# Softmax numerators divided ahead of their transposes, and the products with the values column-tiled for two heads

## The chip, the cores and the metric

The kernel runs on one core of one Trainium2 chip. The metric is the time of one execution in device microseconds (us); less is better. The kernel before took 598.86 us, the median of three runs (598.07 to 598.87 us).

## The reference

Two layers of a hybrid block work on a sequence of 256 tokens, 1024 wide, all in float32. Each layer has three mixers side by side: six heads of block attention ("moba", which on 256 tokens is one causal block), four heads of a chunked mLSTM, and six heads of sliding-window attention ("swa", window 128, two key heads, a sink in the softmax). Their outputs go through w_out, and a feed-forward part with a squared ReLU follows. Cut to what matters here:

```python
def moba_attention(q, k, v):            # causal over 256 tokens
    s = einsum('bhqd,bhld->bhql', q, k) * D ** -0.5
    p = softmax(where(k_pos <= q_pos, s, -inf))
    return einsum('bhql,bhld->bhqd', p, v)

def swa_attention(q, k, v, sinks):      # window of 128, q in two blocks
    s = where(mask, einsum('bnqkgd,bnjkd->bnkgqj', qb, kb) * D ** -0.5, -inf)
    p = softmax(concatenate([s, sink]))[..., :-1]
    return einsum('bnkgqj,bnjkd->bnqkgd', p, vb)

def hybrid_layer(x, ...):
    hn = rms_norm(x, ln1); proj = hn @ w_in      # q, k, v of all mixers
    ...
    x = x + concatenate([y_moba, y_mlstm, y_swa]) @ w_out
    return x + square(relu(rms_norm(x, ln2) @ w_up)) @ w_down
```

## The kernel before

**Large products.** Each float32 product with a weight matrix is made as three passes in a reduced format (fp32r): both operands are split into a high part and the rest, and `three` (L734) issues high times high, high times rest, rest times high (L736, L737, L738). A weight piece comes in by DMA as `raw`; `split` (L289) writes its high part `whi` on ScalarE (L267) and the rest `wlo` on VectorE (L274). There are 8 `whi` and 7 `wlo` buffers, so the splits run ahead of TensorE by at most that much.

**Attention.** `pair` (L1227) handles two heads: six pairs in each layer, three swa and three moba. It makes the scores of both heads in two banks of PSUM (L1249, plain float32, two row tiles of 64 rows side by side). For 256 queries and 256 keys only three of four blocks of 128 are needed, so a head's scores are 128x384: block (0,0), then (1,0) and (1,1). `head` (L1296) then masks and scales them and takes the row's extreme on VectorE (L1312, two instructions a head, called ISA in the order of instructions), takes the exponential on ScalarE with the sum of each row as a by-product (L1318), transposes the three blocks on TensorE (`to_T`, L805, L813) and copies them back to SBUF on ScalarE (L1329). With both heads there, `values` (L1263) multiplies the transposed numerators, as stationary operand, with the values of 64 columns: six products a pair (L1269). The result has the queries on partitions, so the division comes behind it: one reciprocal (L1281) and one product on VectorE (L1284, recorded as L274, out of PSUM); for swa the sinks are added to the sums before. Then two transposes (L813) turn the result, and `split` writes it as high part and rest (`fh`, `fl`) for w_out.

**The rest of a layer.** `mix` (L1336) multiplies with w_out: four results of 128x512, each over eight pieces in the order 3, 4, 5, 6, 7, 0, 1, 2 (the mLSTM's, swa's, moba's). Behind it `turn_both` (L697) transposes the new x (L708) for the feed-forward part, and `hT`, `lT` are its two parts. In the first layer `small_loads` (L586) then loads the second layer's small table by DMA into `tab` and makes `cg` and `sg` from it on VectorE (L597).

**What sets the order.** Nothing is ordered at run time. `Scheduler.run` (L164) builds the program: each piece of work is a generator that yields operations with an engine and a cost in us, and the planner issues the one that can start first by its own clock. Among those that are ready within a few hundredths of a us the lowest rank goes first. Two rules touch the change. Before a long operation on ScalarE or VectorE it looks a little ahead for an urgent one (rank of -25 or less), L213 to L218. An operation with an alternative engine takes the one that ends first, with 0.3 us of favour for the first (`choose`, L95). For TensorE a change of tile mode counts as 0.2 us. Each engine executes its list in order, so an instruction that waits holds all behind it.

Of the kernel before, what the change touches and what calls it, by code (L numbers as in the profile page):

```python
# [14 lines left out]
AF = mybir.ActivationFunctionType  # L15
# [6 lines left out]
HD = 64  # L22
# [113 lines left out]
class Scheduler:  # L136
# [27 lines left out]
    def run(self):  # L164
        while self.threads:
# [47 lines left out]
            if eng in ("ACT", "DVE") and op.cost > 0.3 and th.rank() > URGENTLY:  # L213

                soon = [c for c in ready if c[2].engine == eng and c[1].rank() <= URGENTLY
                        and t < c[0] < min(t + 0.5, t + op.cost - 0.2)]
                if soon:
                    t, th, op = min(soon, key=lambda c: c[0])  # L218
# [25 lines left out]
def tile_hybrid_block(ctx: ExitStack, tc: tile.TileContext, x, xT, smalls, w_in, w_out, w_up,  # L244
# [28 lines left out]
    def tt(waits, o, a, b, op):  # L273
        return dve(waits, free_size(o), lambda: V.tensor_tensor(o, a, b, op=op), bank=bank_of(a, b))  # L274
# [11 lines left out]
    def pe(waits, cost, fn, tiles=""):  # L286
        return Op("PE", cost, waits, fn, tiles=tiles)
# [317 lines left out]
    def small():  # L605
        i, t = yield Get(SMALL)
        return i, SMALL.tiles[i], t
# [237 lines left out]
    class Layer:  # L845
# [381 lines left out]
        def pair(self, swa, i, gate, prio):  # L1227
# [3 lines left out]

# [24 lines left out]
            i4, sums, t4 = yield from small()  # L1256
            for n, (h, (ip, _)) in enumerate(zip(heads, banks)):
                sch.add(prio + h, self.head(swa, h, n, pT, sums, done, ip, max(t, t4)))
# [4 lines left out]
            def values():  # L1263
                for qb in range(2):
                    for n, h in enumerate(heads):
                        d = (n if swa else h) * HD
                        for kb in range(qb + 1):
                            c = (qb + kb) * 128
                            T.matmul(yps[:, qb * 128 + n * HD:qb * 128 + n * HD + HD],  # L1269
                                     MID.tiles[pT[h]][:, c:c + 128], vv[kb][:, d:d + HD],  # L1270
                                     start=kb == 0, stop=kb == qb)

            t = yield pe([done, ty, vev], 0.68, values).ranked(prio)
# [4 lines left out]
            w = [t]  # L1278
            if swa:
                w = [t, (yield tt([done], sums[:, 0:4], sums[:, 0:4], sums[:, 4:8], OP.add))]  # L1280
            tr = yield dve(w, 16, lambda: V.reciprocal(sums[:, 0:4], sums[:, 0:4]))  # L1281
            im, tm = yield Get(MID)
            y = MID.tiles[im][:, 0:256]
            t = yield tt([t, tr, tm], y.rearrange("p (g d) -> p g d", d=HD),  # L1284
                         yps[:, 0:256].rearrange("p (g d) -> p g d", d=HD),
                         sums[:, 0:4, None].to_broadcast([128, 4, HD]), OP.mult)
            PS.put(iy, t)
            SMALL.put(i4, t)
            iy, ps, t = yield from to_T(t, y, 2)
            MID.put(im, t)  # L1290
            hi, lo, ty = yield from self.y_tile(c)
            t = yield from split([t, ty], hi, lo, ps[:, 0:256])
# [3 lines left out]
        def head(self, swa, h, n, pT, sums, done, ip, t):  # L1296
# [5 lines left out]
            nm = sm[:, 0:2]  # L1302
# [14 lines left out]
            for k, cut in enumerate(cuts):  # L1317
                t = yield act([tk], p[:, cut], p[:, cut], AF.Exp, bias=nm[:, k:k + 1],  # L1318
                              scale=-1.0, accum_out=sums[:, 2 * k + n:2 * k + n + 1])
            te = t  # L1320
            if swa:
                es = sums[:, 4:8].rearrange("p (b n) -> p b n", n=2)
                te = yield act([tk], es[:, :, n], nm, AF.Exp,
                               bias=tab[self.l][:, T_SINK + h:T_SINK + h + 1])
            SMALL.put(i, te)
# [6 lines left out]
            done.signal(max(t, te))  # L1332
# [361 lines left out]
```

## Time and profile before

| | |
|---|---|
| median of three runs | 598.86 us |
| time of the profiled execution | 598.18 us |
| its span, first to last instruction | 596.4 us |
| TensorE (PE) busy | 587.6 us, 99% |
| VectorE (DVE) busy | 523.2 us, 88% |
| ScalarE (ACT) busy | 382.3 us, 64% |
| granted TensorE clock | 1.000 |

PE is the matrix engine, PEld its weight loads, which run beside the products. An operation has a line of the kernel, the tiles that it writes and reads (`ps` is a bank of PSUM), and its shape. A float32 product is two records in the profile, because it is done in two passes; a transpose and an fp32r product are one. A matmul's recorded time includes its way through the array, so the distance between two starts says what it costs, not its length. Idle time stands in brackets, with what ended it. Attention lies at about 60 to 115 us in the first layer and 348 to 410 us in the second; each is followed by the feed-forward part.

### The profile page before, as it was taken

To read this page: it belongs to the slowest core of one execution; us is meant where nothing else is said; L and a number is where in the kernel's file an instruction comes from. 1 tells how busy PE (TensorE), PEld (TensorE's weight loads), DVE (VectorE), ACT (ScalarE), POOL (GpSimd) and SP (SyncE) were. 2 spreads that over 40 slices of the span, in tenths; PEclk is the share of its full clock that TensorE was granted. 3 is DMA by queue.
4 is the path that set the end of the run, shared out by engine and by line. 5 is a ranking of instruction groups with operands and counts; after the bars stand their busy time and mean duration, and the time that the engine had idled before them with its cause. 6 is when DMAs were issued, how large, how long until landed. Compare 5 with 4: busy or idle time off the path is not lost.

```text
span 596.4 us, 11480 instructions
## 1 busy us (share of the span) xinstructions
PE 587.6 (99%) x4327; PEld 550.4 (92%) x4327; DVE 523.2 (88%) x1153; ACT 382.3 (64%) x745; POOL 6.8 (1%) x14
## 2 busy tenths in 40 slices
PE   8999999989999999999999999999999999999997
PEld 6999998889999999999999999988999999999996
DVE  6899988389998998989899999875999998998995
ACT  6956887567574656546586778865766555555560
POOL 4000000000000000000000000000000000000000
PEclk9999999999999999999999999999999999999999
DMA  9937236255766466565555453353536556566422
GB/s 318 355 87 241 72 124 199 67 161 177 232 205 210 171 210 209 162 207 198 154 156 161 125 165 126 105 180 109 208 143 225 199 185 211 171 202 218 145 71 71
DMA packets 40967, 103.48 MB, mean 174 GB/s; under 512 B 3568, under 2 KB 17648, under 8 KB 40912
## 3 DMA queue, kind: packets, MB, share of 16 engines
q1 hardware_dynamic: 40496, 102.21, 52.6%
q8 instruction: 34, 0.56, 0.4%
q0 software_dynamic: 128, 0.40, 0.2%
q10 hardware_dynamic: 288, 0.15, 0.1%
q14 instruction: 21, 0.17, 0.1%
HBM read 101.69 MB, written 1.05 MB: 172 GB/s over the span
## 4 chain that ended last, share of the span: by engine, by line
PE 93%; ACT 2%; DMA 2%; DVE 1%; SPq 0%; issue 0%; DVEq 0%; ACTq 0%
PE ps L736 28%; PE ps L738 28%; PE ps L737 28%; PE ps L813 3%; PE ps L1269 3%; PE ps L1249 2%; DMA xs<-in_x_dram 1%; ACT whi L267 1%; DMA mid<-in_xT_dram 1%; DVE wlo L274 1%; ACT tmp L267 1%; PE ps L1056 1%; ACT hT L267 0%; DVE xs L274 0%; PE ps L1031 0%; PE ps L1078 0%
## 5 line engine op out<-in xcount | busy, mean ns | idle before, releaser
L274 DVE TENSOR_TENSOR wlo<-raw,whi 128x1024 fp32r<-128x1024 f32 (+4 forms) x240 | 223.8, 951 | 6.4 <-ACT whi L267 4.4
L267 ACT ACTIVATE whi<-raw 128x1024 fp32r<-128x1024 f32 (+4 forms) x240 | 189.5, 838 | 1.7 <-DMA raw<-in_w_in_dram 1.2
L738 PE MATMUL ps<-hT,wlo 128*128 128x256 f32 x576 | 161.4, 280 | 1.5 <-DVE wlo L274 1.5
L736 PE MATMUL ps<-hT,whi 128*128 128x256 f32 x576 | 162.1, 281 | 0.0
L737 PE MATMUL ps<-lT,whi 128*128 128x256 f32 x576 | 161.6, 281 | 0.0
L736 PE MATMUL ps<-whi,fh 128*128 128x256 f32 (+1 forms) x418 | 140.9, 337 | 0.0
L738 PE MATMUL ps<-whi,fl 128*128 128x256 f32 (+1 forms) x418 | 138.8, 332 | 0.0
L737 PE MATMUL ps<-wlo,fh 128*128 128x256 f32 (+1 forms) x418 | 138.8, 332 | 0.0
L738 PEld LDWEIGHTS ps<-hT,wlo 128*128 128x128 f32 x576 | 108.6, 188 | 1.8 <-DVE wlo L274 1.8
L736 PEld LDWEIGHTS ps<-hT,whi 128*128 128x128 f32 x576 | 108.6, 188 | 0.9
L737 PEld LDWEIGHTS ps<-lT,whi 128*128 128x128 f32 x576 | 108.5, 188 | 0.8
L738 PEld LDWEIGHTS ps<-whi,fl 128*128 128x128 f32 x418 | 78.6, 188 | 8.3
L736 PEld LDWEIGHTS ps<-whi,fh 128*128 128x128 f32 x418 | 78.7, 188 | 6.8 <-issue 0.7
L737 PEld LDWEIGHTS ps<-wlo,fh 128*128 128x128 f32 x418 | 78.7, 188 | 6.2
L267 ACT ACTIVATE arena<-ps 128x512 f32<-128x512 f32 (+3 forms) x52 | 26.3, 515 | 86.7 <-PE ps L738 81.6
L736 PE MATMUL ps<-whi,hT 128*128 128x256 f32 (+2 forms) x256 | 79.9, 312 | 0.7 <-ACT whi L267 0.6
L737 PE MATMUL ps<-wlo,hT 128*128 128x256 f32 (+2 forms) x256 | 76.1, 297 | 1.2 <-DVE wlo L274 1.2
L738 PE MATMUL ps<-whi,lT 128*128 128x256 f32 (+2 forms) x256 | 75.6, 295 | 0.0
L267 ACT ACTIVATE fh<-arena 128x1024 fp32r<-128x1024 f32 x32 | 34.0, 1062 | 48.2 <-DVE arena L274 44.4
L274 DVE TENSOR_TENSOR arena<-arena 128x128 f32<-128x128 f32 (+1 forms) x158 | 55.8, 360 | 4.5 <-ACT arena L267 3.7
L736 PEld LDWEIGHTS ps<-whi,hT 128*128 128x128 f32 x256 | 48.2, 188 | 3.4 <-issue 1.7
L737 PEld LDWEIGHTS ps<-wlo,hT 128*128 128x128 f32 x256 | 48.3, 189 | 2.1 <-DVE wlo L274 2.1
(141 smaller groups left out, 687.3 us busy)
## 6 DMA issues: line engine op xcount, KB each, us to landing
raw<-in_w_up_dram SPq DMA_DIRECT2D x64, 512.0 KB, 4.6
raw<-in_w_down_dram SPq DMA_DIRECT2D x64, 512.0 KB, 4.3
raw<-in_w_in_dram SPq DMA_DIRECT2D x24, 512.0 KB, 4.7
raw<-in_w_out_dram SPq DMA_DIRECT2D x16, 512.0 KB, 3.4
raw<-in_w_in_dram SPq DMA_DIRECT2D x16, 384.0 KB, 3.9
raw<-in_w_in_dram SPq DMA_DIRECT2D x7, 520.0 KB, 5.1
xs<-in_x_dram SPq DMA_DIRECT2D x2, 512.0 KB, 7.2
mid<-in_xT_dram SPq DMA_DIRECT2D x7, 128.0 KB, 5.5
```

The source lines that it names most:

```text
L267: lambda: A.activation(o, i, func, **kw), bank)
L274: return dve(waits, free_size(o), lambda: V.tensor_tensor(o, a, b, op=op), bank=bank_of(a, b))
L736: T.matmul(ps, s[0], m[0], start=start, stop=False)
L737: T.matmul(ps, s[0], m[1], start=False, stop=False)
L738: T.matmul(ps, s[1], m[0], start=False, stop=stop)
L813: T.transpose(ps[:, cs], src[:, cs], ident)
L1056: T.matmul(PS.tiles[ip][:, o], lqk[b, 2 + c, ks], lqk[b, c, qs], start=o.start == 0, stop=o.start > 0)
L1249: T.matmul(PS.tiles[ip][:, o], qT[b, i, q], kT[b, kc, k], start=o.start == 0, stop=o.start > 0)
L1269: T.matmul(yps[:, qb * 128 + n * HD:qb * 128 + n * HD + HD], MID.tiles[pT[h]][:, c:c + 128], vv[kb][:, d:d + HD], start=kb == 0, stop=kb = ...
```

## The change

The sum of a row's exponentials is now used before the transposes. Each head takes its two reciprocals (for swa, after adding the sink's exponentials), multiplies both parts of its numerators by them, on VectorE or, where that ends sooner by the planner's clock, on ScalarE, and only then transposes. The product with the values swaps its operands: the values (64 columns) are stationary, the transposed probabilities move, and the two heads write partitions 0 to 63 and 64 to 127 of one bank, each in a column tile of its own. The result so has the head's dimension on partitions, as w_out wants it: the division behind, its buffer and the two transposes are gone, and `split` reads the bank. The cost that the planner takes for the product stays 0.68 us; the tile mode "columns" is new to it, so that each change to and from it counts as 0.2 us. The look-ahead for urgent operations is cut from 0.5 to 0.3 us, and the least remainder raised from 0.2 to 0.3 us.

```diff
@@ Scheduler.run
                 soon = [c for c in ready if c[2].engine == eng and c[1].rank() <= URGENTLY
-                        and t < c[0] < min(t + 0.5, t + op.cost - 0.2)]
+                        and t < c[0] < min(t + 0.3, t + op.cost - 0.3)]
@@ pair
-            i4, sums, t4 = yield from small()
-            for n, (h, (ip, _)) in enumerate(zip(heads, banks)):
-                sch.add(prio + h, self.head(swa, h, n, pT, sums, done, ip, max(t, t4)))
+            for h, (ip, _) in zip(heads, banks):
+                sch.add(prio + h, self.head(swa, h, pT, done, ip, t))
...
             def values():
-                for qb in range(2):
+                for o, blk, cols in ((slice(0, 256), 0, slice(0, 256)),
+                                     (slice(128, 256), 1, slice(256, 384))):
                     for n, h in enumerate(heads):
                         d = (n if swa else h) * HD
-                        for kb in range(qb + 1):
-                            c = (qb + kb) * 128
-                            T.matmul(yps[:, qb * 128 + n * HD:qb * 128 + n * HD + HD],
-                                     MID.tiles[pT[h]][:, c:c + 128], vv[kb][:, d:d + HD],
-                                     start=kb == 0, stop=kb == qb)
-
-            t = yield pe([done, ty, vev], 0.68, values).ranked(prio)
+                        T.matmul(yps[64 * n:64 * n + 64, o], vv[blk][:, d:d + HD],
+                                 MID.tiles[pT[h]][:, cols], start=blk == 0, stop=blk == 1)
+
+            t = yield pe([done, ty, vev], 0.68, values, "columns").ranked(prio)
...
-            w = [t]
-            if swa:
-                w = [t, (yield tt([done], sums[:, 0:4], sums[:, 0:4], sums[:, 4:8], OP.add))]
-            tr = yield dve(w, 16, lambda: V.reciprocal(sums[:, 0:4], sums[:, 0:4]))
-            im, tm = yield Get(MID)
-            y = MID.tiles[im][:, 0:256]
-            t = yield tt([t, tr, tm], y.rearrange("p (g d) -> p g d", d=HD),
-                         yps[:, 0:256].rearrange("p (g d) -> p g d", d=HD),
-                         sums[:, 0:4, None].to_broadcast([128, 4, HD]), OP.mult)
-            PS.put(iy, t)
-            SMALL.put(i4, t)
-            iy, ps, t = yield from to_T(t, y, 2)
-            MID.put(im, t)
             hi, lo, ty = yield from self.y_tile(c)
-            t = yield from split([t, ty], hi, lo, ps[:, 0:256])
+            t = yield from split([t, ty], hi, lo, yps[:, 0:256])
@@ head
             for k, cut in enumerate(cuts):
                 t = yield act([tk], p[:, cut], p[:, cut], AF.Exp, bias=nm[:, k:k + 1],
-                              scale=-1.0, accum_out=sums[:, 2 * k + n:2 * k + n + 1])
-            te = t
+                              scale=-1.0, accum_out=su[:, k:k + 1])
             if swa:
-                es = sums[:, 4:8].rearrange("p (b n) -> p b n", n=2)
-                te = yield act([tk], es[:, :, n], nm, AF.Exp,
-                               bias=tab[self.l][:, T_SINK + h:T_SINK + h + 1])
-            SMALL.put(i, te)
+                te = yield act([tk], es, nm, AF.Exp, bias=tab[self.l][:, T_SINK + h:T_SINK + h + 1])
+                t = yield tt([te, t], su, su, es, OP.add)
+            t = yield dve([t], 16, lambda: V.reciprocal(su, su))
+            tn = []
+            for k, cut in enumerate(cuts):
+                a, b = p[:, cut], su[:, k:k + 1]
+                tn.append((yield ts([t], a, a, b, None, OP.mult).either(
+                    act([t], a, a, AF.Copy, scale=b))))
+            t = max(tn)
+            SMALL.put(i, t)
             it, pt, t = yield from to_T(t, p, 3)
...
-            done.signal(max(t, te))
+            done.signal(t)
```

Over the whole program TensorE has 48 products for the values where 72 stood, and 24 transposes fewer. VectorE gets 24 reciprocals for 12, 12 additions of the sinks for 6, and 42 of the 48 scalings, and loses 12 products out of PSUM; ScalarE gets the other 6 scalings. The lists of SyncE and GpSimdE are the same as before. On TensorE nothing moves ahead of the first layer's attention; in the attention and the feed-forward part's start of both layers much is ordered anew, and different buffers are used.

**TensorE, the last moba pair of the first layer.** `mid_78` and `mid_79` are the transposed numerators of its two heads (after: `mid_83` and `mid_79`), `arena` holds the values, `fh`, `fl` are the mixers' results. Before:

```order
L1269 MATMUL ps_65<-arena,mid_78 128x64
L1269 MATMUL ps_65<-arena,mid_79 128x64
L1269 MATMUL ps_65<-arena,mid_78 128x64 x2
L1269 MATMUL ps_65<-arena,mid_79 128x64 x2
L736 MATMUL ps_70<-whi_93,fh_107 128x512
L737 MATMUL ps_70<-wlo_104,fh_107 128x512
L738 MATMUL ps_70<-whi_93,fl_111 128x512
L736 MATMUL ps_70<-whi_94,fh_108 128x512
L737 MATMUL ps_70<-wlo_105,fh_108 128x512
L738 MATMUL ps_70<-whi_94,fl_112 128x512
L813 MATMUL ps_66<-ident,mid_84 128x128 x2
```

The same place now:

```order
L1266 MATMUL ps_65<-mid_83,arena 64x256
L1266 MATMUL ps_65<-mid_79,arena 64x256
L1266 MATMUL ps_65<-mid_83,arena 64x128
L1266 MATMUL ps_65<-mid_79,arena 64x128
L736 MATMUL ps_67<-whi_99,fh_107 128x512
L737 MATMUL ps_67<-wlo_103,fh_107 128x512
L738 MATMUL ps_67<-whi_99,fl_111 128x512
L736 MATMUL ps_70<-whi_95,fh_108 128x512
L737 MATMUL ps_70<-wlo_106,fh_108 128x512
L738 MATMUL ps_70<-whi_95,fl_112 128x512
```

Six products became four, and the two transposes of the divided result (`mid_84`) are gone.

**VectorE, the same pair's softmax.** The ISA rows mask the scores and take the row's extreme; `small` holds extremes, sums and reciprocals. Before, it goes on with the division of the pair ahead and with weight splits:

```order
L1312 ISA mid_82,small_118<-ps_65,masks,rq_m 128x256
L1312 ISA small_118 128x1
L1312 ISA mid_83,small_132<-ps_66,masks,rq_m 128x256
L1312 ISA small_132 128x1
L1281 RECIPROCAL small_134<-small_134 128x4
L274 TENSOR_TENSOR mid_84<-ps_65,small_134 128x256
L274 TENSOR_TENSOR wlo_104<-raw_88,whi_92 128x1024
```

Now:

```order
L1295 ISA mid_80,small_125<-ps_65,masks,rq_m 128x256
L1295 ISA small_125 128x1
L1306 RECIPROCAL small_124<-small_124 128x2
L278 TENSOR_SCALAR mid_76<-mid_76,small_124 128x128
L278 TENSOR_SCALAR mid_76<-mid_76,small_124 128x256
L1306 RECIPROCAL small_125<-small_125 128x2
L278 TENSOR_SCALAR mid_80<-mid_80,small_125 128x128
L278 TENSOR_SCALAR mid_80<-mid_80,small_125 128x256
L274 TENSOR_TENSOR fl_111<-ps_66,fh_107 128x256
L274 TENSOR_TENSOR wlo_104<-raw_88,whi_92 128x1024
```

Each head has a reciprocal and two scalings behind its exponentials, and the rest of an earlier pair's result (`fl_111`) and a weight split are queued behind them.

**VectorE, the start of the first layer's feed-forward part.** `lT` is the rest of the turned x, `wlo_101` the fourth weight piece that TensorE needs there, and `cg` is made from the second layer's table. Before:

```order
L283 SCALAR_TENSOR_TENSOR lT<-ps_66,tab,hT 128x256 x2
L274 TENSOR_TENSOR small_133<-small_133 128x1
L274 TENSOR_TENSOR arena<-raw_89 128x256
L278 TENSOR_SCALAR stat_148<-small_133 128x1
L597 SCALAR_TENSOR_TENSOR cg<-rope_t,tab 128x128
L274 TENSOR_TENSOR wlo_101<-raw_86,whi_96 128x1024
```

Now:

```order
L283 SCALAR_TENSOR_TENSOR lT<-ps_65,tab,hT 128x256
L283 SCALAR_TENSOR_TENSOR lT<-ps_63,tab,hT 128x256
L274 TENSOR_TENSOR wlo_101<-raw_86,whi_96 128x1024
L278 TENSOR_SCALAR stat_148<-stat_148 128x1
L274 TENSOR_TENSOR arena<-raw_90,arena 128x256
L274 TENSOR_TENSOR wlo_102<-raw_87,whi_97 128x1024
L597 SCALAR_TENSOR_TENSOR cg<-rope_t,tab 128x128
```

The splits into `wlo_101` and `wlo_102` now stand ahead of the first `cg`.

More of the change, by code (lines that the diff above doesn't have):

```diff
@@ L1277, in pair, with head @@
             gate.put(ig, t)
-            w = [t]
-            if swa:
-                w = [t, (yield tt([done], sums[:, 0:4], sums[:, 0:4], sums[:, 4:8], OP.add))]
-            tr = yield dve(w, 16, lambda: V.reciprocal(sums[:, 0:4], sums[:, 0:4]))
-            im, tm = yield Get(MID)
-            y = MID.tiles[im][:, 0:256]
-            t = yield tt([t, tr, tm], y.rearrange("p (g d) -> p g d", d=HD),
-                         yps[:, 0:256].rearrange("p (g d) -> p g d", d=HD),
-                         sums[:, 0:4, None].to_broadcast([128, 4, HD]), OP.mult)
-            PS.put(iy, t)
-            SMALL.put(i4, t)
-            iy, ps, t = yield from to_T(t, y, 2)
-            MID.put(im, t)
             hi, lo, ty = yield from self.y_tile(c)
-            t = yield from split([t, ty], hi, lo, ps[:, 0:256])
+            t = yield from split([t, ty], hi, lo, yps[:, 0:256])
             PS.put(iy, t)
             self.y[c].signal(t)
-        def head(self, swa, h, n, pT, sums, done, ip, t):
+        def head(self, swa, h, pT, done, ip, t):
             ps = PS.tiles[ip]
@@ L1301, in head @@
             i, sm, t0 = yield from small()
-            nm = sm[:, 0:2]
+            nm, su, es = sm[:, 0:2], sm[:, 2:4], sm[:, 4:6]
             cuts = (slice(0, 128), slice(128, 384))
```

## The prediction

> **What bounds the kernel now.** I read the page's head and its chain first, then what TensorE waits for.
>
> ```profile
> span 596.4 us, 11480 instructions
> PE 587.6 (99%) x4327; PEld 550.4 (92%) x4327; DVE 523.2 (88%) x1153; ACT 382.3 (64%) x745; POOL 6.8 (1%) x14
> PE 93%; ACT 2%; DMA 2%; DVE 1%; SPq 0%; issue 0%; DVEq 0%; ACTq 0%
> PE ps L738 <- DVE wlo L274: 1.5, 1, 1.5
> ```
>
> TensorE is busy for 99% of the span and is 93% of the chain that ended last. The answer on TensorE's waits has five rows, the longest is shown; none names an attention line (L813, L1249, L1269). So inside attention TensorE waits for nobody, and what its list there loses or gains is lost or gained at the end, as long as no wait comes in. What its pieces cost, the chain in order of time and the timeline of TensorE say:
>
> ```profile
> 61.71 1.51 PE ps L1249 x16
> 64.65 0.86 PE ps L1249 x8
> 80.45 1.28 PE ps L1269 x12
> 81.74 0.33 PE ps L813 x3
> ```
>
> ```profile
> 64.37 0.28 PE L738 MATMUL ps<-whi,lT 128*128 128x256 f32 x1
> 64.58 0.93 PE L1249 MATMUL ps<-arena 64*128 64x128 f32 x8
> 65.44 0.39 PE L736 MATMUL ps<-whi,hT 128*128 128x256 f32 x1
> 65.66 0.28 PE L737 MATMUL ps<-wlo,hT 128*128 128x256 f32 x1
> ...
> 77.89 0.37 PE L736 MATMUL ps<-whi,hT 128*128 128x256 f32 x1
> 78.09 0.29 PE L737 MATMUL ps<-wlo,hT 128*128 128x256 f32 x1
> 78.22 0.29 PE L738 MATMUL ps<-whi,lT 128*128 128x256 f32 x1
> ```
>
> A pair's values take 1.28 us (twelve records), a transpose 0.33/3 = 0.11 us. Of the weight products of 256 columns each starts 0.13 us behind the last (78.09 to 78.22), but the second behind a plain float32 group starts 0.20 us behind the first (77.89 to 78.09): leaving such a group costs 0.07 us, 0.08 with the rounding. Behind the row-tiled scores it is 0.22 us (65.44 to 65.66), and the scores start 0.21 us behind the last weight product (64.37 to 64.58): entering a tile mode costs about 0.09 us, leaving it 0.10.
>
> **What goes from TensorE.** Twelve pairs of values: 12 x 1.28 = 15.4 us. The 24 transposes of the results: 24 x 0.11 = 2.6 us. In the lists of both programs a run of weight products follows something else 81 times before and 69 times after: 12 x 0.08 = 1.0 us. Together 19.0 us.
>
> **What comes.** No row shows column tiles. The nearest is the scores: the same two heads, the same 256 and 128 moving columns, two tiles side by side, eight records. One pair takes 0.86 us and two pairs 1.51 us, so a pair streams for 1.51 - 0.86 = 0.65 us, and 0.21 us come once for a group. That gives the bounds for one new group: 0.65 us where even the 0.21 is hidden, 0.86 us as the scores, and 0.65 + 0.65 + 0.21 = 1.51 us where the two heads' tiles take turns. I take 0.86, since streams, heads and passes are those of the scores: 12 x 0.86 = 10.3 us. Entering and the dearer leaving, 0.09 + 0.02 us in twelve places at most: 1.3 us (none, if column tiles switch for free). From the Trainium skill, "TensorE: Matmul & The Clock Gate", section "Measured speedup vs the span model": three column tiles gained 2.38 times, 0.79 of their number; by that, as an estimate, two tiles would take 1.30/1.59 = 0.82 us of streaming beside the 0.21, and the sum would come out 2 us higher.
>
> So TensorE's own list shrinks by 19.0 - 10.3 - 1.3 = 7.4 us.
>
> **The stall at the first layer's feed-forward part.** The one long wait is this, in the timelines of TensorE and of VectorE:
>
> ```profile
> 129.51 0.28 PE L737 MATMUL ps<-lT,whi 128*128 128x256 f32 x1
> 131.33 0.39 PE L738 MATMUL ps<-hT,wlo 128*128 128x256 f32 x1 [1.55 <-DVE wlo L274]
> ```
>
> ```profile
> 126.25 0.86 DVE L283 SCALAR_TENSOR_TENSOR lT<-ps,tab,hT 128x256 fp32r<-128x256 f32 x2
> ...
> 129.85 0.29 DVE L597 SCALAR_TENSOR_TENSOR cg<-rope_t,tab 128x128 f32<-128x128 f32 x1 [2.27 <-DMA tab<-in_smalls_dram]
> 130.06 1.22 DVE L274 TENSOR_TENSOR wlo<-raw,whi 128x1024 fp32r<-128x1024 f32 x1
> ```
>
> VectorE stands 2.27 us at the first `cg`, which waits for the table's DMA, and the split that TensorE needs is queued behind it. TensorE starts 131.33 - 129.51 = 1.82 us later instead of 0.13, so 1.7 us are lost. In the new order that split and the next stand ahead of `cg`. The table's DMA lands 129.85 - 127.11 = 2.7 us behind the last `lT`; in the new list VectorE has two splits and two small operations there, about 1.2 + 1.2 + 0.4 us, so `cg` hardly waits. Late next is `wlo_101` itself. Its new row stands behind two transposed halves and two other splits, but TensorE has 12 weight products of the last mix (12 x 0.24 us, by the distance of 512-wide starts further below, 107.69 to 107.93) between the transposes, which it lacked before. I take 1.5 of the 1.7 us as won, with 0 and 1.9 as ends.
>
> **What is longer in the softmax.** A head's transposes now wait for a reciprocal and two scalings, for swa for the sink's exponential and an addition as well. The groups of instructions price them by the nearest shapes:
>
> ```profile
> L278 DVE TENSOR_SCALAR tmp<-tmp,tab 128x256 f32<-128x256 f32 x8 | 3.2, 402 | 0.0
> L1281 DVE RECIPROCAL small<-small 128x4 f32<-128x4 f32 x12 | 2.0, 171 | 2.3 <-ACT mid L267 2.3
> L274 DVE TENSOR_TENSOR small<-small 128x4 f32<-128x4 f32 x6 | 0.9, 152 | 0.0
> L267 ACT ACTIVATE small<-small,tab 128x2 f32<-128x2 f32 x12 | 3.4, 284 | 0.0
> ```
>
> The scaling of 256 is at most 0.40 us (that row has two per-row operands, the new one has one), that of 128 lies between the 0.15 us of the smallest operations and 0.40; I take 0.28. A moba head's chain grows by 0.17 + 0.28 + 0.40 = 0.85 us, a swa head's by 0.28 + 0.15 more, 1.3 us. What covers it can be read at the first layer's last pair, where least other work is left:
>
> ```profile
> 107.69 0.40 PE L737 MATMUL ps<-wlo,fh 128*128 128x512 f32 x1
> 107.93 0.39 PE L738 MATMUL ps<-whi,fl 128*128 128x512 f32 x1
> ...
> 111.27 0.49 PE L813 MATMUL ps<-ident,mid 128*128 128x128 f32 x3
> ```
>
> ```profile
> 109.82 0.18 ACT L267 ACTIVATION_READ_ACCUMULATOR mid<-mid,small 128x1 f32 x1
> ```
>
> The second head is ready at 109.82 + 0.18 = 110.00, and its transposes start 1.27 us later: 0.85 us would fit without moving anything. And it moves: in the new list twelve 512-wide products and one values group lie between this pair's scores and its first transposes, 12 x 0.24 + 1.06 = 3.9 us, where 12 x 0.24 + 0.1 = 3.0 us lay. Elsewhere the new transposes are put later by similar amounts. On VectorE the reciprocal that waits for the exponentials has `fl_111` and a weight split queued behind it, but there VectorE stood idle for 4.25 us:
>
> ```profile
> 114.47 0.42 DVE L274 TENSOR_TENSOR mid<-ps,small 128x256 f32<-128x256 f32 x1 [4.25 <-PE ps L1269]
> ```
>
> I charge 0.5 us for single short waits, 0 to 3 us.
>
> VectorE's load: 42 scalings by 0.34 us on the mean, 12 reciprocals by 0.17 and 6 additions by 0.15 more, less 12 of the products out of PSUM above by 0.42: 14.3 + 2.0 + 0.9 - 5.0 = 12 us, 6 in each layer. These stages of the first layer hold it:
>
> ```profile
> 60.00:75.00 15.00, 15.00 (x127) 13.91 (x125) 14.96 (x73) 13.07 (x49) 0.00 (x0) 1.00 0.23 75
> 75.00:90.00 15.00, 15.00 (x132) 14.13 (x130) 12.92 (x43) 13.40 (x41) 0.00 (x0) 1.00 0.39 134
> 90.00:105.00 15.00, 15.00 (x100) 12.94 (x96) 12.51 (x36) 10.60 (x31) 0.00 (x0) 1.00 0.61 193
> 105.00:115.00 10.00, 10.00 (x58) 8.02 (x57) 2.47 (x11) 4.57 (x13) 0.00 (x0) 1.00 0.09 34
> ```
>
> The fourth number is VectorE's: idle 2.1 + 2.5 + 7.5 = 12 us from 75 to 115 us, twice what is added; only from 60 to 75 is it full. I count nothing. The look-ahead alone moves nothing on TensorE ahead of attention and is in the order read above: nothing either.
>
> **The sum.** -7.4 - 1.5 + 0.5 = -8.4 us against the profiled execution's 598.18 us: 589.8 us. The median before lies 0.68 us above that execution; I give 590.0.
>
> **The rivals.**
> 1. *The column tiles take turns.* Both tiles use all rows of the array. Then a group takes 1.51 us, 12 x 0.65 = 7.8 us more: 597.6 us, about what it was. For it: nothing here shows two column tiles at once. Against: two row tiles do run at once. The Trainium skill, "TensorE: Matmul & The Clock Gate", section "The mechanism", speaks for it: weight loads pass running matmuls only where the row group differs, and here it doesn't. The trace disagrees, in groups:
>
> ```profile
> L1269 PE MATMUL ps<-arena,mid 128*128 128x64 f32 x144 | 17.4, 270 | 0.0
> L1269 PEld LDWEIGHTS ps<-arena,mid 128*128 128x128 f32 x144 | 17.3, 191 | 0.4
> ```
>
> Loads and products on all 128 rows fill 17.3 and 17.4 us, but one pair's twelve are through in 1.28 us, 15.4 us for all: they overlap. Chance 0.12.
> 2. *The longer softmax takes TensorE's place.* In-order TensorE stands at each head's transposes until VectorE has scaled. The 24 heads' chains grow by 12 x 0.85 + 12 x 1.3 = 26 us; the change turns into a loss once more than 8.9/24 = 0.37 us a head stay uncovered, and with half of it uncovered the time is 598.18 - 8.9 + 13 = 602.3 us. Against: the 1.27 us above, and the order. Chance 0.08.
> 3. *VectorE's added work comes too early for its idle time.* It is full from 60 to 75 us; if the 6 us a layer push the weight splits into TensorE's way, all 12 come back: 589.8 + 12 = 601.8 us. It decides where the splits are less than 6 us ahead. Against: VectorE later runs out of work (2.47 of 10 us), so the splits are then as far ahead as their buffers let them. Chance 0.05.
>
> My forecast has 0.75.
>
> **How the numbers follow.** The forecast's own ends: with 0.65 us a group (-2.5), free switching (-1.3), 586.0; with the stall kept (+1.5) and 3 us of waits (+2.5), 593.8. For 8 in 10 part of the rivals is needed, as 0.25 us a head uncovered (+6): 586 to 596. A measurement of this kernel tells 0.2%, 1.2 us, from no change. Faster: the forecast 0.75, and milder forms of the rivals, 0.04 + 0.02 + 0.02, together 0.83. Same: 0.08 of rival 1. Slower: 0.06 + 0.03 = 0.09.
>
> **What would show it.** Right: eight records of values per pair in 0.86 us (0.65 to 0.9), starts in pairs; no wait of TensorE on L813 beyond 0.5 us in all; no 1.5 us wait for `wlo` behind 120 us; a span of about 588 us. Rival 1 would show as 1.5 us a pair and starts one by one; rival 2 as waits of L813 for L278; rival 3 as waits for `wlo` in attention. Wrong altogether would be a loss in the feed-forward part, whose order changes little.

## The result and the profile after

| | before | after |
|---|---|---|
| median of the runs on one chip | 598.87 us (598.07 to 599.72, 4 runs) | 588.68 us (588.53 to 589.14, 4 runs) |
| profiled execution, its span | 598.18, 596.4 us | 588.58, 586.8 us |
| TensorE busy | 587.6 us | 579.8 us |
| VectorE busy | 523.2 us | 528.1 us |

The ratio is 0.9831 [0.9814, 0.9848]: the change is 1.7% faster. The prediction said 590.0 us (586 to 596).

The page's head after, its chain by engine, and TensorE's waits (the whole answer):

```profile
span 586.8 us, 11358 instructions
PE 579.8 (99%) x4255; PEld 538.9 (92%) x4255; DVE 528.1 (90%) x1200; ACT 384.9 (66%) x752; POOL 6.8 (1%) x14
PE 95%; DMA 3%; DVE 1%; SPq 0%; issue 0%; ACT 0%; DVEq 0%
```

```profile
PE ps L557 <- DVE mid L551: 1.1, 1, 1.1
PE ps L736 <- ACT whi L267: 0.7, 1, 0.7
PE ps L737 <- DVE wlo L274: 0.6, 2, 0.4
PE ps L737 <- DVE lT L283: 0.4, 1, 0.4
PE ps L879 <- DVE stat L283: 0.2, 1, 0.2
```

TensorE still sets the end. The 1.5 us wait of L738 is gone, no attention line is among the waits, and one wait is new: L737 for `lT`. The chain in order of time shows the new values (L1266, in before L1269 with 1.28 us) beside the scores (L1248):

```profile
81.58 1.45 PE ps L1266 x16
85.01 0.80 PE ps L1266 x8
85.81 0.86 PE ps L1248 x8
```

A pair takes 0.80 us; two pairs behind each other take 1.45 us, so a pair streams for 0.65 us. In the trace its eight records start in four couples, 7 ns apart within a couple: at 0, 7, 267, 274, 483, 490, 592 and 599 ns.

The start of the first layer's feed-forward part, on TensorE and on VectorE:

```profile
116.08 1.03 PE L708 MATMUL ps<-ident,xs 128*128 128x128 f32 x8
...
121.11 1.04 PE L708 MATMUL ps<-ident,xs 128*128 128x128 f32 x8
```

```profile
124.28 1.21 DVE L274 TENSOR_TENSOR wlo<-raw,whi 128x1024 fp32r<-128x1024 f32 x1
125.81 1.21 DVE L274 TENSOR_TENSOR wlo<-raw,whi 128x1024 fp32r<-128x1024 f32 x1
127.18 0.29 DVE L597 SCALAR_TENSOR_TENSOR cg<-rope_t,tab 128x128 f32<-128x128 f32 x1 [0.17 <-DMA tab<-in_smalls_dram]
```

The two splits now stand ahead of `cg`, which waits 0.17 us for the table instead of 2.27. The transposes come in two halves, and the 24 weight products between them (12 of the last mix, 12 of the feed-forward part) hide the `lT` of the first half.

The new wait lies at the same place of the second layer, where the 16 transposes stand together. On TensorE and on VectorE:

```profile
405.83 1.93 PE L708 MATMUL ps<-ident,xs 128*128 128x128 f32 x16
407.51 0.36 PE L736 MATMUL ps<-hT,whi 128*128 128x256 f32 x1
408.30 0.39 PE L737 MATMUL ps<-lT,whi 128*128 128x256 f32 x1 [0.42 <-DVE lT L283]
```

```profile
406.63 1.22 DVE L274 TENSOR_TENSOR wlo<-raw,whi 128x1024 fp32r<-128x1024 f32 x1
407.77 3.22 DVE L283 SCALAR_TENSOR_TENSOR lT<-ps,tab,hT 128x256 fp32r<-128x256 f32 x8
```

A weight split of 1.22 us stands ahead of the eight `lT`. The second product starts 0.79 us behind the first instead of 0.12: 0.67 us lost.

**Where the time went.** I added the distances between starts on TensorE by kind of instruction, in both traces, so that each distance counts for the instruction that begins it:

| | first layer | second layer | both |
|---|---|---|---|
| values (L1269 to L1266) | -3.0 | -2.8 | -5.8 |
| transposes (L813) | -0.7 | -1.2 | -1.9 |
| transposes of the new x (L708) | -0.4 | -0.3 | -0.8 |
| the stall behind 129 us | -1.7 | | -1.7 |
| the new stall at 407.5 us | | +0.7 | +0.7 |
| other weight products | -0.5 | -0.3 | -0.8 |
| together | -6.3 | -3.9 | -10.2 |

Ahead of the first scores, which the change does not touch, this execution lost 0.6 us; that part took 60.6 to 61.8 us in the traces of this case. The spans so differ by 9.6 us.

VectorE's work between 60 and 115 us, of before and of after, the fourth number:

```profile
60.00:115.00 55.00, 55.00 (x408) 49.00 (x406) 42.85 (x161) 41.64 (x131) 0.00 (x0) 1.00 0.35 116
```

```profile
60.00:115.00 55.00, 55.00 (x393) 46.09 (x393) 49.80 (x191) 45.23 (x138) 0.00 (x0) 1.00 0.41 135
```

It grew by 7.0 us there, and 5.2 of its 12.2 us of idle time are left. ScalarE has 3.6 us more. These 55 us are fixed, though, and attention now ends about 4 us earlier, so some later work has moved in. What the change itself gives VectorE is read from the groups of instructions:

```profile
L278 DVE TENSOR_SCALAR mid<-mid,small 128x256 f32<-128x256 f32 x20 | 7.0, 348 | 0.0
L278 DVE TENSOR_SCALAR mid<-mid,small 128x128 f32<-128x128 f32 x22 | 6.2, 283 | 0.2
```

The scalings take 13.2 us, the reciprocals 1.8 us and the additions 1.0 us more than before, and the products out of PSUM (5.1 us) are gone: 10.9 us, 5.4 in each layer.

### The profile page after: what moved, and what is told of

Same layout as the page of the kernel before. It is cut to its first block, busy times and chain, and to the rows that moved or that the text cites. A ratio compares the mean times of both kernels' runs of the same rounds, so it can differ in the third digit from the quotient of the medians.

```text
span 586.8 us, 11358 instructions
## 1 busy us (share of the span) xinstructions
PE 579.8 (99%) x4255; PEld 538.9 (92%) x4255; DVE 528.1 (90%) x1200; ACT 384.9 (66%) x752; POOL 6.8 (1%) x14
## 4 chain that ended last, share of the span: by engine, by line
PE 95%; DMA 3%; DVE 1%; SPq 0%; issue 0%; ACT 0%; DVEq 0%
PE ps L736 29%; PE ps L737 29%; PE ps L738 29%; DMA raw<-in_w_in_dram 3%; PE ps L813 2%; PE ps L1248 2%; PE ps L1266 2%; PE ps L708 1%; PE ps L1056 1%; SPq L294 0%; PE ps L1031 0%; PE ps L1078 0%; PE ps L1077 0%; DVE wlo L274 0%; PE ps L678 0%; PE ps L1076 0%
## 5 line engine op out<-in xcount | busy, mean ns | idle before, releaser
L737 PE MATMUL ps<-lT,whi 128*128 128x256 f32 x576 | 161.5, 280 | 0.4 <-DVE lT L283 0.4
L738 PE MATMUL ps<-hT,wlo 128*128 128x256 f32 x576 | 161.2, 280 | 0.0
L737 PE MATMUL ps<-wlo,fh 128*128 128x256 f32 (+1 forms) x418 | 138.8, 332 | 0.0
L738 PE MATMUL ps<-whi,fl 128*128 128x256 f32 (+1 forms) x418 | 138.8, 332 | 0.0
L737 PEld LDWEIGHTS ps<-lT,whi 128*128 128x128 f32 x576 | 108.5, 188 | 1.6 <-DVE lT L283 0.6
L738 PEld LDWEIGHTS ps<-hT,wlo 128*128 128x128 f32 x576 | 108.7, 189 | 0.0
L738 PEld LDWEIGHTS ps<-whi,fl 128*128 128x128 f32 x418 | 78.6, 188 | 8.2
L737 PEld LDWEIGHTS ps<-wlo,fh 128*128 128x128 f32 x418 | 78.7, 188 | 6.2
L737 PE MATMUL ps<-wlo,hT 128*128 128x256 f32 (+2 forms) x256 | 76.7, 299 | 0.7 <-DVE wlo L274 0.6
L738 PE MATMUL ps<-whi,lT 128*128 128x256 f32 (+2 forms) x256 | 76.2, 298 | 0.0
L274 DVE TENSOR_TENSOR arena<-arena 128x128 f32<-128x128 f32 (+1 forms) x157 | 55.5, 358 | 10.6 <-ACT arena L267 10.2
L737 PEld LDWEIGHTS ps<-wlo,hT 128*128 128x128 f32 x256 | 49.0, 191 | 1.7 <-DVE wlo L274 1.4
```

The source lines that it names most:

```text
L737: T.matmul(ps, s[0], m[1], start=False, stop=False)
L738: T.matmul(ps, s[1], m[0], start=False, stop=stop)
```

## The experiments

My theory: TensorE's own list sets the end; two column tiles run side by side; the stall of the first layer is a matter of the order on VectorE; the longer softmax is covered. The rivals: the column tiles take turns; the softmax's length, or VectorE's load, eats the gain. Each kernel is the changed one with one edit, unless it says otherwise; every ratio is against the kernel before on the same chip. What a kernel takes more than the change is the difference of medians; some are from other chips, where the kernel before took 598.94 to 599.25 us (598.87 us beside the change).

**The heads one behind the other** (`heads_in_turn`). All products of the first head stand ahead of those of the second.

```diff
-                for o, blk, cols in (...):
-                    for n, h in enumerate(heads):
+                for n, h in enumerate(heads):
+                    for o, blk, cols in (...):
```

> The changed kernel with the four products of a pair in another sequence: both of the first head, then both of the second; the order of everything else is the same. In the changed kernel the heads alternate and a group takes 0.80 us. If two column tiles run side by side only where neighbours in TensorE's list are of different tiles, the first head's 128-wide product and the second's 256-wide one are the only ones that can overlap: a group takes 0.80 + 0.65 - 0.22 = about 1.2 us, 12 x 0.4 = 5 us more, 593.5 us. If each tile takes its instructions from the queue by itself, the group stays at 0.80 us and the time at 588.7 us (within 0.5).

Measured: 589.00 us, 0.9827 [0.9811, 0.9843], as the change. The chain of its trace:

```profile
81.59 1.50 PE ps L1266 x16
85.08 0.81 PE ps L1266 x8
```

The eight starts lie at 0, 13, 266, 280, 482, 496, 591 and 605 ns: four couples again, and the first four records have 256 columns, the last four 128. In the program each head has 256, 256, 128, 128, and the second head's stand behind all of the first's. So the second head's first product starts ahead of the first head's last ones: the tiles overlap whatever the sequence of the program.

**Both heads in one column tile** (`one_column_tile`). Both write partitions 0 to 63, the second head into the other half of the bank, and its result is left out of what follows.

```diff
-                        T.matmul(yps[64 * n:64 * n + 64, o], vv[blk][:, d:d + HD], ...,
-                                 start=blk == 0, stop=blk == 1)
+                        T.matmul(yps[0:64, 256 * n + o.start:256 * n + o.stop], vv[blk][:, d:d + HD], ...,
+                                 start=blk == n == 0, stop=blk == n == 1)
```

> The changed kernel with both heads in the same column tile (partitions 0 to 63, the second head in the other half of the bank), in the same order; the second head's product is not used. My theory: the gain hangs on the two tiles running at once, so a group takes 0.80 + 0.65 = 1.45 us and the time is 588.7 + 12 x 0.65 = 596.5 us (595.5 to 597.5). The rival, that the gain comes from fewer weight loads and not from two tiles at once: a group of 0.8 to 0.9 us and 588.7 to 590 us.

Measured: 596.51 us, 0.9958 [0.9943, 0.9973]. In its chain:

```profile
81.30 2.74 PE ps L1266 x16
86.02 1.45 PE ps L1266 x8
```

A pair takes 1.45 instead of 0.80 us, and the eight records start one by one (0, 267, 483, 698, 914, 1023, 1133, 1242 ns). Twelve pairs by 0.64 us (1.444 less 0.801) are 7.7 us; the median rose by 7.8. The order of TensorE, VectorE, ScalarE and GpSimd is the change's, row for row, and so is the number of weight loads. With that, what rival 1 would have been worth is shown, and that it did not happen: most of the change's gain hangs on the tiles running side by side.

**The division ahead alone** (`divided_ahead_only`). The old products and the two transposes of the result are back, with a plain copy by ScalarE in the place of the division behind.

```diff
-            t = yield pe([done, ty, vev], 0.68, values, "columns").ranked(prio)
+            t = yield pe([done, ty, vev], 0.68, values).ranked(prio)
...
+            t = yield act([t, tm], y, yps[:, 0:256], AF.Copy)
+            iy, ps, t = yield from to_T(t, y, 2)
```

> The changed kernel's softmax (divided ahead of the transposes) with the old products: six a pair, queries on partitions, a plain copy on ScalarE in place of the division behind, and the two transposes of the result. My theory: TensorE's list is that of before, so the time is that of before, less at most the 1.7 us of the stall at the first layer's feed-forward part: 597 to 599.5 us. The rival, that the shorter end of a pair or the division's place is worth something by itself: under 595 us. The rival that the longer softmax costs TensorE waits: over 601 us.

Measured: 603.77 us, 1.0080 [1.0063, 1.0098]: slower than before by 4.7 us. My theory (597 to 599.5 us) missed, and the rival of the longer softmax came. TensorE has the products and transposes of before, in another order; what is added are waits, most of them at the two places where attention ends:

```profile
120.56 0.50 PE L736 MATMUL ps<-whi,fh 128*128 128x512 f32 x1 [0.72 <-ACT fh L267]
121.88 0.50 PE L738 MATMUL ps<-whi,fl 128*128 128x512 f32 x1 [0.59 <-DVE fl L274]
126.08 0.98 PE L708 MATMUL ps<-ident,xs 128*128 128x128 f32 x7 [0.44 <-DVE xs L274]
```

So the longer softmax is not free here. My reading is that the change carries it because its other half takes the copy or division and the two transposes out of the last pair's way; which of these does it, and how much of the loss is the planner's new order, is not shown. From this kernel to the change 15.1 us are won, of which the values and the 24 transposes themselves, by the table above, are 7.7.

**Two more scalings on VectorE** (`scaled_twice`), by 1.0, in each head's way ahead of its transposes.

```diff
+            for cut in cuts:
+                t = yield ts([t], p[:, cut], p[:, cut], 1.0, None, OP.mult)
```

> The changed kernel with each head's two scalings followed by two more, by 1.0, on VectorE: each head's softmax is longer by 0.28 + 0.35 = 0.63 us, and VectorE has 24 x 0.5 = 12 us more. My theory: the chain lies beside other products on TensorE, and the order leaves room for it: 588.7 to 590 us. The rival, that the longer softmax is paid by TensorE: 24 x 0.63 = 15 us, 603 us; half of it, 596 us, would show that the change itself has paid about as much for its own 0.85 to 1.3 us a head.

Measured: 596.69 us, 0.9955 [0.9937, 0.9973]: 8.0 us more than the change. My theory (588.7 to 590 us) missed. TensorE in the first layer, and the added scalings:

```profile
116.87 0.86 PE L1266 MATMUL ps<-mid,arena 128*64 128x256 f32 x6 [0.35 <-ACT mid L267]
118.20 0.50 PE L736 MATMUL ps<-whi,fh 128*128 128x512 f32 x1 [0.47 <-ACT fh L267]
119.91 0.50 PE L738 MATMUL ps<-whi,fl 128*128 128x512 f32 x1 [0.97 <-DVE fl L274]
122.31 1.93 PE L708 MATMUL ps<-ident,xs 128*128 128x128 f32 x16
125.43 0.38 PE L737 MATMUL ps<-lT,whi 128*128 128x256 f32 x1 [1.08 <-DVE lT L283]
```

```profile
L278 DVE TENSOR_SCALAR mid<-mid 128x128 f32<-128x128 f32 (+1 forms) x48 | 11.9, 251 | 0.0
```

A scaling by 1.0 is shorter than the change's own scalings by a value for each row (0.22 and 0.28 us for 128 and 256 columns, instead of 0.28 and 0.35), so a head has 0.50 us more, not the 0.63 us of the expectation, and VectorE 12 us. That is enough to bring waits. It does not show, as the expectation would have it, that the change itself paid as much: none of these waits is in its trace but one for `lT`, in the other layer. Whether the chain or VectorE's 12 us cost the time was open, so four kernels took the two apart.

**The extra work beside the chain** (`extra_aside`). The same two scalings, behind the transposes, as a thread of its own.

```diff
+            def aside(t, im=im, p=p):
+                for cut in cuts:
+                    t = yield ts([t], p[:, cut], p[:, cut], 1.0, None, OP.mult)
+                MID.put(im, t)
+            sch.add(0, aside(t))
```

> The changed kernel with the two more scalings by 1.0 per head on VectorE, but behind the transposes, as work of its own that nothing waits for (the numerators' buffer comes free later by it): 48 operations, 15 us of VectorE, none of it in a head's chain. If VectorE's load cost the 8 us of the kernel that scaled twice: 594 to 597 us. If the chain did: 589 to 591 us.

Measured: 594.27 us, 0.9916 [0.9897, 0.9934], 5.6 us more than the change, at the load theory's lower edge. VectorE (the fourth number) from 90 to 105 us, in the change and here:

```profile
90.00:105.00 15.00, 15.00 (x91) 11.50 (x90) 13.07 (x43) 12.47 (x35) 0.00 (x0) 1.00 0.63 206
90.00:105.00 15.00, 15.00 (x87) 11.39 (x83) 14.97 (x57) 9.16 (x26) 0.00 (x0) 1.00 0.49 171
```

It was full from 60 to 90 us already; now it is full to 105, and in `scaled_twice` too (15.00 of 15). The numerators' buffer also comes free later here, and what that costs is not told apart from the load.

**A longer chain without VectorE or ScalarE** (`longer_on_gpsimd`).

```diff
+            a = p[:, cuts[0]]
+            t = yield Op("POOL", 0.5, [t], lambda a=a: G.tensor_scalar(a, a, 1.0, None, op0=OP.mult))
```

> The changed kernel with one more operation in each head's softmax, ahead of its transposes: a scaling by 1.0 of the first 128 columns, on GpSimd, which does nothing else at that time. By an estimate from GpSimd's float32 operations in this trace (0.43 us for writing 384 columns, 1.5 us for a scaling of 512 integers on four rows) it takes 0.3 to 0.6 us, and the chain grows by 0.5 to 0.9 us with the way there and back, without a microsecond more for VectorE or ScalarE. If the chain has room in the changed kernel and the two engines' load is what costs: 588 to 590 us. If the length of the chain costs by itself: about half of the 8 us of the kernel that scaled twice, 592 us or more.

Measured: 593.74 us, 0.9915 [0.9898, 0.9931], 5.1 us more than the change: "592 us or more", the side of the chain. But its trace says something else. The GpSimd group, then two places of TensorE and one of VectorE:

```profile
L1314 POOL TENSOR_SCALAR mid<-mid 128x128 f32<-128x128 f32 x24 | 15.8, 660 | 376.8 <-DVE mid L278 355.3 <-PE ps L813 15.3 <-PE ps L738 5.8
```

```profile
121.25 0.98 PE L708 MATMUL ps<-ident,xs 128*128 128x128 f32 x7 [1.02 <-DVE xs L274]
...
140.75 0.39 PE L738 MATMUL ps<-hT,wlo 128*128 128x256 f32 x1 [1.28 <-DVE wlo L274]
```

```profile
127.61 0.29 DVE L597 SCALAR_TENSOR_TENSOR cg<-rope_t,tab 128x128 f32<-128x128 f32 x1 [2.75 <-DMA tab<-in_smalls_dram]
```

In the new order `cg` stands ahead of the splits again and waits 2.75 us; from there VectorE is busy without a gap up to the split for which TensorE waits 1.28 us. L708 takes 1.2 us more. Attention's own lines hardly wait. Nor is VectorE left quite as it was: the planner gives it all 48 divisions here, 42 in the change.

**The extra work on ScalarE** (`extra_on_scalar`), two copies of the numerators in the chain.

```diff
+            for cut in cuts:
+                t = yield act([t], p[:, cut], p[:, cut], AF.Copy)
```

> The changed kernel with two more operations in each head's softmax, ahead of its transposes, as when VectorE scaled twice (596.7 us against 588.7), but on ScalarE: plain copies of the numerators onto themselves, about 0.8 us a head. The chain in front of the transposes grows as there or a little more, VectorE gets no more work. If the chain was what cost the 8 us: 596 us or more. If it was VectorE's load: 589 to 591 us.

Measured: 592.51 us, 0.9885 [0.9859, 0.9910], 3.8 us more than the change: between the two. It is no clean test of the chain either: the copies take 0.41 and 0.31 us, and ScalarE is busy for 14.78 and 14.68 us of the 15 from 75 and from 90 us, where the change has 13.84 and 12.47.

**The extra work in the last pair alone** (`scaled_twice_last`), the lines of `scaled_twice` under `if not swa and h >= 4`.

> The changed kernel with the two more scalings per head on VectorE in the last pair of each layer alone, four heads of 24, ahead of their transposes. If what the kernel that scaled twice lost was lost at the end of attention, where TensorE waits for the last pair and nothing else is left to do (2.5 of its 5.8 us in the first layer stand there in its trace), the two layers lose about as much here: 592 to 594 us. If the load of VectorE from 75 to 105 us is what counts, a sixth of the 8 us: 589 to 590.5 us.

Measured: 590.53 us, 0.9863 [0.9848, 0.9878], 1.8 us more than the change: nearer to a sixth of the 8 us than to all of it. And nearly all of the loss stands behind attention, where the order put the 16 transposes together again:

```profile
118.69 2.17 PE L708 MATMUL ps<-ident,xs 128*128 128x128 f32 x16
120.62 0.36 PE L736 MATMUL ps<-hT,whi 128*128 128x256 f32 x1
121.88 0.39 PE L737 MATMUL ps<-lT,whi 128*128 128x256 f32 x1 [0.89 <-DVE lT L283]
```

To part attention from what follows, I took two distances of the first layer from each trace: from the first scores to the last L708, and from there to the first L678, the transposes with which the feed-forward part ends. Where 12 feed-forward products lie ahead of the last L708, as in the change (1.4 us), they are counted to the second.

| first layer, us more than the change | attention | feed-forward part |
|---|---|---|
| the change itself | 58.2 | 169.4 |
| `scaled_twice` | +4.0 | +1.8 |
| `extra_aside` | +2.4 | +1.0 |
| `longer_on_gpsimd` | +2.0 | +2.7 |
| `extra_on_scalar` | +3.4 | +0.9 |
| `scaled_twice_last` | +0.2 | +1.6 |
| the kernel before | +4.3 | +2.0 |

So neither theory stands by itself. In this attention VectorE's load alone costs 2.4 us and a longer chain alone 2.0 us (of which 1.2 us are L708's), and both together 4.0. The second layer's attention adds 0.5, 1.2 and 1.8 us, in the same sequence: over both layers 2.9 and 3.1, together 5.9. The first layer's feed-forward part loses 0.9 to 2.7 us in each of these kernels, although nothing in it was edited, with waits at places that the planner ordered anew: for `lT` in three of them, for the split behind `cg` in `longer_on_gpsimd`, short ones for `wlo` in `extra_on_scalar`. From the second layer's last L708 to the end the five lie between 1.2 us less and 0.5 us more. These are single executions (that of `scaled_twice` is 1.4 us faster than its median), and `heads_in_turn`, with the change's order row for row, takes 0.7 us more in the first feed-forward part, in one wait for `wlo`: so much can be chance. What stays open is how much of a kernel's loss is the edit and how much the order that the planner finds for it: an edit of the softmax that keeps the order fixed was not made.

**All divisions on ScalarE** (`scalings_on_scalar`).

```diff
-                tn.append((yield ts([t], a, a, b, None, OP.mult).either(
-                    act([t], a, a, AF.Copy, scale=b))))
+                tn.append((yield act([t], a, a, AF.Copy, scale=b)))
```

> The changed kernel with all 48 divisions of the numerators on ScalarE; the planner put 42 of them on VectorE. VectorE is relieved of 13 us, a head's chain grows by about 0.1 to 0.25 us. TensorE's waits in the changed kernel add up to about 3 us, of which 1.5 lie behind attention, so by my theory there is little to win: 588 to 591 us. If VectorE's load still costs the changed kernel something: below 587.5 us.

Measured: 593.51 us, 0.9906 [0.9886, 0.9926], 4.8 us worse than the change, a miss for both expectations. ScalarE is full then, 14.68 and 14.84 of 15 us (VectorE as well up to 90 us, but not behind it, 10.23), and TensorE waits for it:

```profile
75.00:90.00 15.00, 13.52 (x111) 12.20 (x112) 14.77 (x50) 14.68 (x49) 0.00 (x0) 1.00 0.51 173
90.00:105.00 15.00, 14.91 (x98) 10.23 (x94) 10.23 (x39) 14.84 (x47) 0.00 (x0) 1.00 0.42 140
```

```profile
PE ps L1266 <- ACT mid L267: 1.9, 2, 1.5
```

ScalarE's 66% over the whole kernel hides that from 60 to 105 us the change leaves it 1.2 to 2.5 us in 15 to spare.

**The stall alone** (`before_table_later`): the kernel before, with the planner's cost of the table's DMA set to 900e3 in place of 300e3, so that `cg` moves behind the split.

> The kernel before with a dearer planner's cost for the load of the second layer's table, so that the split for which TensorE waited 1.7 us stands ahead of the operation that waits for the table; nothing else of the change. My theory: that stall is worth its 1.7 us by itself: 597.2 us (ratio to before 0.9972). If TensorE then waits for something else at once, 598.5 to 599 us.

Measured: 597.32 us, 0.9976 [0.9965, 0.9988]. By the medians 1.8 us are won, by the ratio 1.4; the first layer of its trace is 1.3 us shorter. The wait of L738 is down to 0.2 us. The stall is worth about what the trace of before said (1.7 us), without any of the rest of the change.

**The old look-ahead** (`old_lookahead`): 0.5 and 0.2 us, as before, in the changed kernel.

> The changed kernel with the look-ahead of before (0.5 and 0.2 us). In the kernel before, the new look-ahead alone leaves the order of all engines as it is; in the changed kernel it changes the order from the first layer's feed-forward part on. In the changed kernel TensorE loses 0.67 us at the start of the second layer's feed-forward part, where a weight split of 1.22 us stands on VectorE ahead of the rests of the turned x. If the shorter look-ahead lets that split go ahead, this kernel is 0.5 to 1 us faster, 587.9 us (ratio to the changed kernel 0.9985). If the look-ahead does nothing for the time: 588.7 us within 0.3.

Measured: 589.81 us, 0.9841 [0.9827, 0.9855]. The `lT` wait is gone, but L708 waits 0.8 us for `xs`, and the first layer takes 1.4 us more. The time lies outside both expectations; with the medians 0.2% apart and the ratios 0.1%, this is at the edge of what can be told. That the new look-ahead costs the change anything is not seen.

**A look-ahead between** (`look_ahead_between`): 0.5 and 0.3 us.

> The changed kernel with a look-ahead of 0.5 us and a least remainder of 0.3 us (the change: 0.3 and 0.3; before: 0.5 and 0.2). Only some 30 rows of the order differ, all at the start of the second layer's feed-forward part: the weight split that stood ahead of the first lT there now stands behind the eight of them. If that split costs the 0.67 us at that place: 588.0 us, 0.1% less, which is at the edge of what can be measured; in the trace TensorE's wait of L737 for lT is then gone and the first two starts of the feed-forward part lie 0.12 us apart. Rival: something else is late there, as xs for L708 was with the old look-ahead: 588.7 us or more.

Measured: 589.00 us, 0.9829 [0.9809, 0.9849]: the rival's case. TensorE's waits:

```profile
PE ps L708 <- DVE xs L274: 0.7, 1, 0.7
```

The wait for `lT` is gone and that for `xs` is in its place. No version measured here is faster than the change beyond the intervals.

## Why the prediction was right, point by point

- **Values.** Predicted 15.4 us out and 10.3 us in, -5.1; measured -5.8. A pair takes 0.80 us, not the 0.86 us of the scores that I took for the nearest: the streaming is the same 0.65 us, what comes once for a group is 0.15 us, not 0.21. By the Trainium skill, "TensorE: Matmul & The Clock Gate", section "Measured speedup vs the span model", three tiles gain 2.38 times; the estimate from it, 0.82 us of streaming for two tiles, is not borne out: one tile takes 1.45 - 0.15 = 1.30 us, two 0.65, all of a factor of two.
- **Transposes.** Predicted -2.6, measured -1.9 between starts, which hold changes of mode and short waits as well.
- **Entries and modes.** Predicted -1.0 and +1.3; the other weight products measured -0.8. Entering does cost about 0.09 us: the first values record starts 0.21 us behind a weight product of 256 columns (0.12 us otherwise), and 0.33 us behind one of 512 (0.23). The mode is no dearer than I took it, but the places are fewer: nine groups of values stand behind a weight product and four ahead of one, about 0.9 us instead of 1.3. The other 0.7 us have no single place in the traces and stay open.
- **L708.** Not in the sum, -0.8: in before the tenth of the sixteen transposes starts 0.40 us behind the ninth in either layer, 0.11 us otherwise; after, no distance of the kind is left. What made that gap is not shown: no wait of L708 is in the answer of before.
- **The first stall.** Predicted -1.5; measured -1.7 in the trace and 1.4 (ratio) to 1.8 us (medians) by itself. `cg` hardly waits, as the step said, and the 12 mix products between the transposes cover what was late next. I did not see the 12 feed-forward products beside them.
- **New waits.** Predicted +0.5 (0 to 3); measured +0.7, one wait, in the second layer's feed-forward part. That place I had not named; a loss in the feed-forward part was what I had put down as wrong altogether.
- **The longer softmax, covered.** Right for the change: L813 is not among TensorE's waits. The reason was incomplete. I took the cover as there and the list's saving as independent of it; `divided_ahead_only` shows that with the old products the same softmax costs 4.7 us net, its new order included.
- **VectorE's added load.** Predicted 6 us a layer into 12 us of idle time, no cost. Measured 5.4 us a layer (a scaling takes 0.31 us on the mean, not 0.34), no wait of TensorE in attention. Another 6.0 us a layer beside the chain (twelve heads by 0.50 us), more than the 5.2 us of idle time left, cost 5.6 us in all. Both fit the budget as I read it.
- **The sum.** -8.4 predicted, -9.6 between the profiled executions, -10.2 between the medians. Carried over to the median, my sum gives 590.5 us; that I gave 590.0 brought it nearer without a reason. TensorE's list without the two stalls makes -9.3 of it, where -7.4 was predicted: values -0.7, entries and modes -1.1, L708 -0.8, transposes +0.7. So the mechanism held, and that the total came so close is in part luck: two terms were off by 0.7 us in opposite ways.

Rival 1 was wrong: the trace speaks against the rule that weight loads pass running matmuls only where the row group differs (Trainium skill, "TensorE: Matmul & The Clock Gate", section "The mechanism"), since here both tiles use all rows and still start 7 ns apart, and the loads of the second couple start 0.05 us behind the first couple's products, which go on to 0.27 us. That section of the Trainium skill also lets a load into a background weight buffer pass; no run here tells whether that is what happens. Rivals 2 and 3 did not come in the change but are near: `scaled_twice`, with 0.50 us more a head, loses 8.0 of its 10.2 us. My threshold of 0.37 us a head for rival 2 counted uncovered time, of which the change's trace shows none in attention.

## What to carry to other kernels

Price a change in a full pipeline by the list of the engine that bounds it, but add for each of the other engines how much idle time the stage itself has left; a share over the whole kernel hides it. A step that moves work ahead of a wait can cost time alone (here 4.7 us) and pay together with one that shortens what comes behind it. Where a planner re-orders everything after an edit, part of a difference of 1 to 3 us can be the new order, and 0.7 us in a single trace came without one: look at the known weak places (here the start of the feed-forward part) before giving it to the edit.

## What the runs showed of the hardware

- Two column tiles of 64 columns, all 128 rows each, run fully side by side in float32: 0.65 us of streaming for both, 1.30 us for the same products in one tile; and it makes next to no difference whether the program alternates the tiles (starts 7 ns apart, 0.80 us) or has both products of one head, four records, ahead of those of the other (13 to 14 ns apart, 0.81 us). In the second case products start in another sequence than the program's: the four records of 256 columns first, then the four of 128.
- A scaling of 128x128 in float32 by 1.0 took 0.66 us on GpSimd on the mean (0.57 in the median, one of 24 took 1.71) and 0.22 us on VectorE. By a value for each row it took VectorE 0.28 us; for 256 columns the two were 0.28 and 0.35 us.
- A change of TensorE from full-array weight products into the column tiles takes about 0.09 us, as much as into the row tiles of the scores.
